# Head norms: sums of squares by two float32r products and 1/sqrt by logarithm, exponential and a Newton step

## The chip, the cores and the metric

The kernel runs on one core of one Trainium2 chip. The metric is the time of one launch in device microseconds (us). The core's engines are written as in the profile: PE is TensorE's matrix multiply and PEld its weight load, DVE is VectorE, ACT is ScalarE, POOL is GpSimd, and SP issues DMAs. Each engine works through its own list of instructions in order; between engines they wait on semaphores.

## What is computed

Four layers on a sequence of 512 tokens with 2048 channels. The first is a block with three branches side by side, then come an attention layer with a state space branch, a forgetting attention layer and a last norm. The change touches the first block alone, in three places, each a norm over the 64 channels of a head:

```python
# rwkv branch, 12 heads of 64: the key is brought to unit length per head
kk = (k * k_k).reshape(B, S, H, N)
kk = kk / jnp.maximum(jnp.sqrt(jnp.sum(jnp.square(kk), axis=-1, keepdims=True)), 1e-12)
...
_, y = lax.scan(step, jnp.zeros((B, H, N, N), f32), xs)
y = y.transpose(1, 0, 2, 3)
# ... and its output is normed per head
mu = jnp.mean(y, axis=-1, keepdims=True)
var = jnp.mean(jnp.square(y - mu), axis=-1, keepdims=True)
y = ((y - mu) * lax.rsqrt(var + GN_EPS)).reshape(B, S, C) * gn_g + gn_b      # GN_EPS = 64e-5
...
# stick-breaking attention, 12 heads of 64: q and k are normed per head
def _rms(x, g):
    y = xf * lax.rsqrt(jnp.mean(jnp.square(xf), axis=-1, keepdims=True) + RMS_EPS)   # 1e-6
q = _rms(heads(q), qn_g).astype(f32) * (HEAD_DIM ** -0.5)
k = _rms(heads(k), kn_g).astype(f32)
```

## The kernel before

Activations lie channel by token: a tile of 128 partitions holds 128 channels (two heads) of all 512 tokens, in float32. A dense product of a layer is a chain of steps, one for each 128 input channels. A step is three matmuls of 128x128 weights by 128x512 activations in float32r, since weights and activations are both split into a high and a low half: L310 is high by high, L311 and L312 are the mixed ones. The weights come from HBM in chunks of four steps (tile wr); the high half wh is a copy on ACT (L180) or on POOL (L279), the low half wl a subtraction on DVE (L162). L162, L175, L177 and L180 are helpers: two-operand arithmetic on DVE, an activation function on ACT without and with a bias operand, and a scaled copy on ACT.

The order of the work is written by Python generators. A dense product yields after each step, and `beside(main, side, wait)` advances a second generator by one piece for each piece of the first, from piece `wait` on. The smaller work of a head is thus dealt out between dense steps, and a `yield` in it means "one more dense step (or so) of the other stream first". What the program writes first stands first in each engine's list; nothing reorders it by cost. The rwkv branch runs six pairs of heads, j = 0 to 5, some 80 us each; `front(j + 1)` is dealt out beside the recurrence of pair j. Then the stick-breaking branch runs six pairs, some 59 us each, in the same manner.

`head_rs` is the function of the change. It takes one or two tiles of squares and a function `use` that applies the result, and it is called 18 times, all between 60 and 890 us of the span:

- six **key calls** (`front`, inside `decay`, one square, HEAD_LAG[0]). Just ahead of them `decay` makes two matmuls (L1398), two Tanh on ACT (L177), a linear step on DVE (L1401), a scan along time on DVE (L1402) and two Exp on ACT (L175); the square was made earlier.
- six **output norms** (`norm`, one square, HEAD_LAG[1]).
- six **stick calls** (`stick_front`, two squares, of q and of k, HEAD_LAG[2]), beside the dense product of v; after that product `turn` transposes v on PE (L1753), beside the product of the gate.

Before, a call makes for each square four float32 matmuls with the squares as weights and the 128x2 tile `heads` as data (L382; a float32 matmul stands in the trace as two records). That gives the sums with tokens on partitions, 8 numbers for each partition and square. On these `newton` works: a shift of the bits and three Newton steps, ten small instructions on DVE. L391 widens them to a full tile, the call yields HEAD_LAG times, and four float32 transposes for each square (L405) turn the tile back, to PSUM, where `use` reads it. Both PSUM tiles come from a ring of two (`early`).

Of the kernel before, what the change touches and what calls it, by code (L numbers as in the profile page):

```python
# [9 lines left out]
F32 = mybir.dt.float32  # L10
# [21 lines left out]
HEAD_LAG = (3,5,7)  # L32
# [108 lines left out]
class Kern:  # L141
# [49 lines left out]
    def constants(self, tmp):  # L191
# [33 lines left out]
        self.heads = c.tile([128, 2], F32, name="heads")  # L225
        V.tensor_copy(self.heads, blk[:, 0:128:64])
        self.ident_r = mr("ident_r")
        self.copy(self.ident_r, self.ident)
        self.one = c.tile([128, 1], F32, name="one")
# [132 lines left out]
    def small(self):  # L362
        return self.ps.tile([128, 512], F32, name="sm", bufs=4)
# [9 lines left out]
    def head_rs(self, pool, ring, sqs, ops, use, lag=4):  # L373


        nc = self.nc
        V = nc.vector
        n = 8 * len(sqs)
        ps = self.early()
        for i, sq in enumerate(sqs):  # L380
            for b in range(4):
                nc.tensor.matmul(ps[:, 8 * i + 2 * b:8 * i + 2 * b + 2], sq[:, 128 * b:128 * b + 128], self.heads,  # L382
                                 start=True, stop=True)
        small = lambda name, dt=F32: pool.tile([128, n], dt, name=name, bufs=2)
        m = small("hm")
        ops(m, ps[:, 0:n])
        y = self.newton(m, small("hy", I32), small("ht"))
        wide = []
        for i in range(len(sqs)):
            wide.append(ring())  # L390
            V.tensor_copy(wide[i].rearrange("p (g c) -> p g c", c=64),  # L391
                          y[:, 8 * i:8 * i + 8, None].to_broadcast([128, 8, 64]))
        for _ in range(lag):
            yield
        for i, t in enumerate(wide):
            ps = self.early()
            for b in range(4):
                n = slice(128 * b, 128 * b + 128)
                self.spread(ps[:, n], t[:, n])
            use(i, ps)  # L400
            yield
# [967 lines left out]
    def rwkv(self, pool, tm, yd, acts, rs):  # L1369
# [9 lines left out]
        def front(j):  # L1379
# [13 lines left out]
            def decay():  # L1393
# [17 lines left out]
                yield from self.head_rs(pool, tm, [sq], lambda m, s: V.tensor_scalar(m, s, 1e-24, None, op0=OP.max), use, HEAD_LAG[0])  # L1411
# [39 lines left out]
        def norm(j, g, bon, gate):  # L1451
# [16 lines left out]
            for _ in range(3):  # L1468
                yield
            yield from self.head_rs(pool, tb, [sq], lambda m, s: V.tensor_scalar(m, s, 1.0 / 64, 64e-5, op0=OP.mult,  # L1470
                                                                            op1=OP.add), use, HEAD_LAG[1])

# [448 lines left out]
```

## Time and profile before

| | |
|---|---|
| Time, median of three runs | 3025.04 us (3021.55 to 3025.70) |
| The profiled execution | 3014.29 us, of it 3012.5 us span |
| Mean granted clock of PE in it | 0.987 |
| PE busy | 97% of the span |
| DVE, ACT, POOL busy | 54%, 38%, 17% |
| The stretch of the 18 calls, 60 to 890 us | PE busy 804.0 us of 830.0 |

The profiled execution ran 10.75 us under the median. Its span goes from the first to the last instruction; 1.8 us lie around it. A row of a timeline gives the start from the span's start, the length, the engine, the line, what is written and read, and in brackets how long the engine stood idle before the row and what ended that. Rows of equal instructions are merged, with their count behind an x; the length is then that of all.

### The profile page before, as it was taken

The numbers are of one execution on the slowest core, as the hardware profiler recorded it, in microseconds if no ns is written. First come the engines' busy times: TensorE is split into PE (matmuls) and PEld (weight loads), VectorE is DVE, ScalarE is ACT, GpSimd is POOL, SyncE is SP. The second block draws the span as 40 slices with busy tenths as digits, with TensorE's granted clock in tenths as the row PEclk, the third lists the DMA queues.
The fourth block names the chain that finished last, engine by engine and source line by source line (L and its number), as shares of the span: only waits on it lengthen the run. The fifth ranks groups of instructions, "written<-read, shape, count | busy, mean of one in ns | idle before, by whom it ended". The sixth has DMA issues, their size and how long they took to land. (4 is left out here: it accounts for less than half of the span.)

```text
span 3012.5 us, 42942 instructions
## 1 busy us (share of the span) xinstructions
PE 2935.8 (97%) x16068; PEld 2400.4 (80%) x16068; DVE 1618.0 (54%) x3140; ACT 1134.9 (38%) x2043; POOL 498.8 (17%) x951
## 2 busy tenths in 40 slices
PE   7999999999999999999999999999999999999998
PEld 5777777878887777788888887878888888888887
DVE  7555555477667665655554456344444444444533
ACT  4444443354454223222344454233333232323432
POOL 4111111014764220211100000111101010100011
PEclk9999999999999999999999999999999999999999
DMA  4212122322235556455433325443333333323443
GB/s 141 64 59 60 55 60 69 95 75 84 90 95 167 155 163 196 133 158 157 138 105 103 104 85 177 147 130 109 101 105 96 98 96 97 95 92 95 147 122 119
DMA packets 195298, 334.03 MB, mean 111 GB/s; under 512 B 29696, under 2 KB 44672, under 8 KB 193936
## 3 DMA queue, kind: packets, MB, share of 16 engines
q1 hardware_dynamic: 193808, 327.08, 35.9%
q0 software_dynamic: 1280, 4.20, 0.4%
q8 instruction: 126, 2.06, 0.3%
q14 instruction: 84, 0.69, 0.1%
HBM read 289.55 MB, written 42.70 MB: 110 GB/s over the span
## 5 line engine op out<-in xcount | busy, mean ns | idle before, releaser
L310 PE MATMUL big<-hi,wh 128*128 128x512 f32 x3440 | 1375.7, 400 | 4.1 <-ACT hi L180 2.9
L312 PE MATMUL big<-hi,wl 128*128 128x512 f32 x3440 | 1350.9, 393 | 7.3 <-DVE wl L162 6.8
L311 PE MATMUL big<-lo,wh 128*128 128x512 f32 x3440 | 1349.1, 392 | 2.3 <-DVE lo L162 2.3
L162 DVE TENSOR_TENSOR wl<-wr,wh 128x512 fp32r<-128x512 f32 x884 | 648.3, 745 | 721.0 <-ACT wh L180 711.7
L312 PEld LDWEIGHTS big<-hi,wl 128*128 128x128 f32 x3440 | 649.6, 189 | 153.5 <-DVE wl L162 15.8
L310 PEld LDWEIGHTS big<-hi,wh 128*128 128x128 f32 x3440 | 649.7, 189 | 150.0 <-issue 10.7
L311 PEld LDWEIGHTS big<-lo,wh 128*128 128x128 f32 x3440 | 650.1, 189 | 133.2 <-DVE lo L162 5.6
L180 ACT ACTIVATE wh<-wr 128x512 fp32r<-128x512 f32 x820 | 505.8, 626 | 632.0 <-PE big L311 515.7
L1231 POOL TENSOR_SCALAR dm<-cb,cq 128x128 f32<-128x128 f32 (+1 forms) x64 | 42.4, 663 | 598.1 <-DVE mx L674 580.1
L680 ACT ACTIVATE pm<-pm,mx 128x128 f32<-128x128 f32 (+3 forms) x128 | 70.5, 552 | 178.1 <-DVE mx L676 178.1
L162 POOL TENSOR_TENSOR ssq<-ssq,sq 128x512 f32<-128x512 f32 (+1 forms) x43 | 54.6, 1269 | 380.1 <-ACT sq L175 359.5
L162 DVE TENSOR_TENSOR tm<-big,rs 128x512 f32<-128x512 f32 x86 | 59.2, 688 | 73.4 <-PE big L312 73.3
L175 ACT ACTIVATE sq<-xn 128x512 f32<-128x512 f32 (+1 forms) x47 | 28.8, 613 | 177.8 <-DVE xn L162 166.3
L279 POOL CAST wh<-wr 128x512 fp32r<-128x512 f32 x64 | 47.7, 747 | 143.5 <-PE big L311 93.0
L180 ACT ACTIVATE pt<-sm 128x512 f32<-128x512 f32 (+3 forms) x96 | 43.4, 526 | 62.7 <-PE sm L708 62.7
L162 DVE TENSOR_TENSOR xn<-big,xr 128x512 f32<-128x512 f32 (+1 forms) x50 | 33.3, 667 | 56.7 <-PE big L312 45.5
L1610 POOL MEMSET xi<- 64x16 f32 x6 | 0.7, 119 | 371.4 <-DVE xi L1609 371.4
L180 ACT ACTIVATE qk<-tm 128x512 fp32r<-128x512 f32 x32 | 20.2, 633 | 96.2 <-DVE tm L1366 48.1
L162 POOL TENSOR_TENSOR ssq<-xn 128x512 f32<-128x512 f32 x3 | 3.1, 1040 | 310.4 <-DMA wr<-w_out_even 143.5
L162 DVE TENSOR_TENSOR pl<-sm,pt 128x512 fp32r<-128x512 f32 (+1 forms) x48 | 25.9, 596 | 44.3 <-ACT pt L180 44.3
L686 DVE TENSOR_SCALAR pm<-pm,sm 128x128 f32<-128x128 f32 (+3 forms) x128 | 43.3, 400 | 1.1
L1366 DVE SCALAR_TENSOR_TENSOR tm<-big,rs 128x512 f32<-128x512 f32 x34 | 23.4, 689 | 36.9 <-PE big L312 36.9
(445 smaller groups left out, 3140.4 us busy)
## 6 DMA issues: line engine op xcount, KB each, us to landing
wr<-w_in_odd SPq DMA_DIRECT2D x256, 256.0 KB, 3.3
wr<-w_in SPq DMA_DIRECT2D x228, 256.0 KB, 3.1
wr<-w_in_even SPq DMA_DIRECT2D x192, 256.0 KB, 3.5
wr<-w_out SPq DMA_DIRECT2D x64, 256.0 KB, 3.8
wr<-w_out_even SPq DMA_DIRECT2D x64, 256.0 KB, 3.4
wr<-w_out_odd SPq DMA_DIRECT2D x64, 256.0 KB, 3.3
xr<-x SPq DMA_DIRECT2D x48, 256.0 KB, 3.0
yl<-y SPq DMA_DIRECT2D x45, 256.0 KB, 3.8
```

Of the source, the lines that this page charges most:

```text
L162: (eng or self.nc.vector).tensor_tensor(out, a, b, op=op)
L175: self.nc.scalar.activation(out, x, f, scale=scale)
L180: self.nc.scalar.activation(out, x, AF.Copy, scale=scale)
L279: self.nc.gpsimd.tensor_copy(wh, wr)
L310: nc.tensor.matmul(ps, wh[:, i], hi, start=(k == 0), stop=False)
L311: nc.tensor.matmul(ps, wh[:, i], lo, start=False, stop=False)
L312: nc.tensor.matmul(ps, wl[:, i], hi, start=False, stop=(k == n - 1))
L680: nc.scalar.activation(d, d, AF.Exp, bias=mx[:, b:b + 1], accum_out=sm[:, b:b + 1])
L686: V.tensor_scalar(d, d, sm[:, b:b + 1], None, op0=OP.mult)
L1231: nc.gpsimd.tensor_scalar(D[:, QOFF[b]:QOFF[b] + n], cb[:, 0:n], -1.0, cq[:, b, h:h + 1], op0=OP.mult, op1=OP.add)
L1366: self.nc.vector.scalar_tensor_tensor(t, ps, scale, rs, op0=OP.mult, op1=OP.mult)
L1610: G.memset(X.rearrange("p i c -> p (i c)")[:, 0:256:17], 1.0)
```

## The change

`head_rs` makes the sums as full tiles. The square is split into a high and a low half (a copy on ACT, a subtraction on DVE, tiles from the caller's ring). The call then yields HEAD_LAG times, and two float32r products of 128x512 with a 128x128 block matrix as weights give the sum (`blk_r`) or the mean (`mean_r`) of a head, spread over its 64 channels, in PSUM. 1/sqrt is exp(-0.5 ln): Ln on ACT (with the floor as bias; for the key calls DVE takes the maximum first), Exp on ACT, and one Newton step as three instructions on DVE, all on 128x512. `use` reads the result from SBUF. The small matmuls, `newton`'s part here, the widening copy and the transposes are gone; HEAD_LAG goes from (3, 5, 7) to (0, 4, 0).

```diff
-HEAD_LAG = (3,5,7)
+HEAD_LAG = (0,4,0)
...
-        self.heads = c.tile([128, 2], F32, name="heads")
-        V.tensor_copy(self.heads, blk[:, 0:128:64])
+        self.mean_r = mr("mean_r")
+        self.copy(self.mean_r, blk, scale=1.0 / 64)
...
-    def head_rs(self, pool, ring, sqs, ops, use, lag=4):
-        ps = self.early()
-        for i, sq in enumerate(sqs):
-            for b in range(4):
-                nc.tensor.matmul(ps[:, 8 * i + 2 * b:8 * i + 2 * b + 2], sq[:, 128 * b:128 * b + 128], self.heads,
-                                 start=True, stop=True)
...
-        m = small("hm")
-        ops(m, ps[:, 0:n])
-        y = self.newton(m, small("hy", I32), small("ht"))
...
+    def head_rs(self, ring, sqs, mat, op, floor, use, lag):
+        V = self.nc.vector
+        parts = []
+        for sq in sqs:
+            parts.append((ring(F32R), ring(F32R)))
+            self.split(*parts[-1], sq)
         for _ in range(lag):
             yield
-        for i, t in enumerate(wide):
-            ps = self.early()
-            for b in range(4):
-                n = slice(128 * b, 128 * b + 128)
-                self.spread(ps[:, n], t[:, n])
-            use(i, ps)
+        first = []
+        for sq, (hi, lo) in zip(sqs, parts):
+            ps = self.sums(self.early(), hi, lo, mat)
+            y, t = sq, ring()
+            if op == OP.add:
+                self.act(y, ps, AF.Ln, bias=self.floors[floor])
+            else:
+                V.tensor_scalar(y, ps, floor, None, op0=op)
+                self.act(y, y, AF.Ln)
+            first.append((ps, y, t))
+        for _, y, _ in first:
+            self.act(y, y, AF.Exp, scale=-0.5)
+        for i, (ps, y, t) in enumerate(first):
+            V.scalar_tensor_tensor(t, y, -0.5, y, op0=OP.mult, op1=OP.mult)
+            V.scalar_tensor_tensor(t, ps, floor, t, op0=op, op1=OP.mult)
+            V.scalar_tensor_tensor(y, t, 1.5, y, op0=OP.add, op1=OP.mult)
+            use(i, y)
             yield
...
-                yield from self.head_rs(pool, tm, [sq], lambda m, s: V.tensor_scalar(m, s, 1e-24, None, op0=OP.max), use, HEAD_LAG[0])
+                yield from self.head_rs(tm, [sq], self.blk_r, OP.max, 1e-24, use, HEAD_LAG[0])
...
+            yield from self.head_rs(tb, [sq], self.mean_r, OP.add, 64e-5, use, HEAD_LAG[1])
...
+            self.head_rs(tm, [y for _, _, _, y in x], self.mean_r, OP.add, 1e-6, use, HEAD_LAG[2]), STICK_WAIT[0])
```

The diff moves the lines of the file by two to four: L310 to L312 of before are L314 to L316 of the changed kernel, L1398 is L1401, L1647 is L1649, L1741 is L1743. Three places in the engines' lists follow. In all of them tm stands for any tile of the ring of that name.

PE at the fourth key call: two matmuls of `decay`, a dense step, and the first PE work of `head_rs`. Before:

```order
L312 MATMUL big<-hi,wl 128x512
L1398 MATMUL pa<-wdad,up 128x512 x2
L310 MATMUL big<-hi,wh 128x512
L311 MATMUL big<-lo,wh 128x512
L312 MATMUL big<-hi,wl 128x512
L382 MATMUL pa<-heads,tm 128x2 x4
L1647 MATMUL sm<-xb,GT 32x32 x32
L310 MATMUL big<-hi,wh 128x512
```

In the changed kernel:

```order
L316 MATMUL big<-hi,wl 128x512
L1401 MATMUL pa<-wdad,up 128x512 x2
L314 MATMUL big<-hi,wh 128x512
L315 MATMUL big<-lo,wh 128x512
L316 MATMUL big<-hi,wl 128x512
L422 MATMUL pa<-tm,blk_r 128x512
L423 MATMUL pa<-tm,blk_r 128x512
L1649 MATMUL sm<-xb,GT 32x32 x32
```

The two products (L422, L423) stand where the four small matmuls (L382) stood, one dense step and no more behind `decay`'s matmuls. Before, the transposes followed three dense steps further on; in the changed kernel nothing more of the call is on PE.

ACT at the same call, before: `decay`'s Tanh pair (L177) and Exp pair (L175), and what follows them:

```order
L180 ACTIVATE wh<-wr 128x512 x2
L177 ACTIVATE tm<-pa,half_w_147 128x512
L177 ACTIVATE tm<-pa,half_a_145 128x512
L175 ACTIVATE tm<-tm 128x512 x2
L180 ACTIVATE xb<-sm,m_110 64x512
L180 ACTIVATE wh<-wr 128x512
L177 ACTIVATE tm<-tm,oka,half_k_a 128x512
```

In the changed kernel:

```order
L180 ACTIVATE wh<-wr 128x512 x2
L177 ACTIVATE tm<-pa,half_w_151 128x512
L177 ACTIVATE tm<-pa,half_a_149 128x512
L175 ACTIVATE tm<-tm 128x512 x2
L180 ACTIVATE tm<-tm 128x512
L175 ACT_TABLE_LOAD
L175 ACTIVATE tm<-tm 128x512
L175 ACT_TABLE_LOAD
L175 ACTIVATE tm<-tm 128x512
L180 ACTIVATE xb<-sm,m_110 64x512
L177 ACTIVATE tm<-tm,oka,half_k_a 128x512
```

The copy of the square's high half (L180, tm from tm) stands behind the Exp pair, and Ln and Exp, each behind a table load, stand ahead of the copy to xb. In the whole of ACT's list table loads go from 31 to 66.

DVE at the fourth stick call, before: from the widening copy (L391) on, with the applications to q and k (L1741), the scores' arithmetic (sbe) and v's product coming out of PSUM (tm from big):

```order
L391 COPY tm<-hy 128x512 x2
L162 TENSOR_TENSOR wl<-wr,wh 128x512
L162 TENSOR_TENSOR sbe<-sbe,sm 128x512 x2
L162 TENSOR_TENSOR sbe<-sbe,sm 128x256
L162 TENSOR_TENSOR wl<-wr,wh 128x512
L162 TENSOR_TENSOR sbe<-sbe,m_lt 128x3x128
L162 TENSOR_TENSOR sbe<-sbe,m_lt 128x128
L1741 SCALAR_TENSOR_TENSOR RKV<-tm,qg_151,pa 128x512
L162 TENSOR_TENSOR q_7760<-RKV,q_7760 64x512
L162 TENSOR_TENSOR q_7763<-RKV,q_7763 64x512
L162 TENSOR_TENSOR tm<-big,rs 128x512
L1741 SCALAR_TENSOR_TENSOR RKV<-tm,pvt,pa 128x512
```

In the changed kernel, from the Newton step for k to the same row of v:

```order
L400 SCALAR_TENSOR_TENSOR tm<-tm 128x512
L401 SCALAR_TENSOR_TENSOR tm<-pa,tm 128x512
L402 SCALAR_TENSOR_TENSOR tm<-tm 128x512
L1743 SCALAR_TENSOR_TENSOR RKV<-tm,pvt 128x512
L162 TENSOR_TENSOR kl_5876<-RKV,k_7518 64x512
L162 TENSOR_TENSOR kl_5877<-RKV,k_7522 64x512
L162 TENSOR_TENSOR sbe<-sbe,sm 128x512 x2
L162 TENSOR_TENSOR sbe<-sbe,sm 128x256
L162 TENSOR_TENSOR wl<-wr,wh 128x512
L162 TENSOR_TENSOR sbe<-sbe,m_lt 128x3x128
L162 TENSOR_TENSOR sbe<-sbe,m_lt 128x128
L162 TENSOR_TENSOR tm<-big,rs 128x512
```

v's product comes out of PSUM (tm from big) behind the whole chain of k, its low halves (kl) and a further piece of the scores' arithmetic; before it stood ahead of k's application. Ahead of the rows shown stand, in the changed kernel, the two low halves of the squares and the same four instructions (L400 to L402, L1743) for q.

## Rows read from the trace of the kernel before

**Rows 1.** The page's first part: busy us (share of the span) xinstructions.

```profile
PE 2935.8 (97%) x16068; PEld 2400.4 (80%) x16068; DVE 1618.0 (54%) x3140; ACT 1134.9 (38%) x2043; POOL 498.8 (17%) x951
```

**Rows 2.** Groups of PE, 60-890 us: count, busy us, mean ns, idle before.

```profile
L382 PE MATMUL pa<-heads,tm 128*128 128x2 f32 x144 | 17.7, 249 | 8.0 <-ACT tm L177 5.5 <-ACT tm L175 2.4
...
L405 PE MATMUL pa<-ident,tm 128*128 128x128 f32 x72 | 11.3, 298 | 0.9 <-DVE tm L391 0.8
...
L382 PE MATMUL pa<-heads,tb 128*128 128x2 f32 x48 | 6.4, 256 | 0.0
...
L405 PE MATMUL pa<-ident,tb 128*128 128x128 f32 x24 | 3.6, 272 | 0.0
```

**Rows 3.** PE's waits, 60 to 890 us: in total, times, longest.

```profile
PE pa L1753 <- DVE tm L162: 2.9, 3, 1.2
```

**Rows 4.** Timeline, fourth key call: start us, length us, instruction [idle before].

```profile
261.06 1.13 PE L1398 MATMUL pa<-wdad,up 64*128 64x512 f32 x4
...
263.50 0.69 ACT L177 ACTIVATE tm<-pa,half_w 128x512 f32<-128x512 f32 x1
...
264.24 1.05 PE L382 MATMUL pa<-heads,tm 128*128 128x2 f32 x8 [1.16 <-ACT tm L177]
...
265.10 0.41 DVE L1401 TENSOR_SCALAR tm<-tm 128x512 f32<-128x512 f32 x1
...
265.54 1.22 DVE L1402 TENSOR_TENSOR_SCAN tm<-reset,tm 128x512 f32<-128x512 bf16 x1
...
266.80 1.29 ACT L175 ACTIVATE tm<-tm 128x512 f32<-128x512 f32 x2 [2.04 <-DVE tm L1402]
```

**Rows 5.** Timeline, the second output norm, just ahead of that call.

```profile
248.70 0.95 PE L382 MATMUL pa<-heads,tb 128*128 128x2 f32 x8
...
250.93 0.63 ACT L180 ACTIVATE wh<-wr 128x512 fp32r<-128x512 f32 x1 [1.81 <-PE big L311]
...
254.36 0.82 ACT L177 ACTIVATE tb<-tb,pvt 128x512 f32<-128x512 f32 x1 [2.80 <-DVE tb L162]
...
257.19 0.68 DVE L162 TENSOR_TENSOR tm<-big,rs 128x512 f32<-128x512 f32 x1
```

**Rows 6.** Groups of ACT and DVE, 60-890 us, columns as in Rows 2.

```profile
L175 ACT ACT_TABLE_LOAD x12 | 15.4, 1283 | 0.2
...
L1741 DVE SCALAR_TENSOR_TENSOR RKV<-tm,pvt,pa 128x512 f32<-128x512 f32 x6 | 4.4, 738 | 0.0
```

**Rows 7.** Timeline: a pair of float32r products over all channels.

```profile
154.08 0.39 PE L419 MATMUL pa<-tm,blk_r 128*128 128x512 f32 x1
...
154.30 0.40 PE L420 MATMUL pa<-tm,blk_r 128*128 128x512 f32 x1
```

**Rows 8.** Timeline: a table load and what follows it on ACT.

```profile
618.20 1.28 ACT L177 ACT_TABLE_LOAD   x1
...
619.49 1.28 ACT L177 ACTIVATE sbl<-sbl 128x1280 f32<-128x1280 f32 x1
```

**Rows 9.** Timeline, fourth stick call.

```profile
748.82 0.61 ACT L175 ACTIVATE tm<-tm 128x512 f32<-128x512 f32 x1
...
749.67 1.84 PE L382 MATMUL pa<-heads,tm 128*128 128x2 f32 x16
...
757.61 1.28 ACT L175 ACTIVATE sbe<-sbe 128x1280 f32<-128x1280 f32 x1 [7.66 <-DVE sbe L162]
...
765.21 0.69 DVE L162 TENSOR_TENSOR tm<-big,rs 128x512 f32<-128x512 f32 x1
...
766.04 0.63 PE L1753 MATMUL pa<-ident,tm 128*128 128x128 f32 x4 [1.21 <-DVE tm L162]
```

**Rows 10.** Timeline, second stick call.

```profile
629.34 1.05 PE L382 MATMUL pa<-heads,tm 128*128 128x2 f32 x8 [1.80 <-ACT tm L175]
...
634.86 0.21 ACT L175 ACTIVATE cn<-s5x 128x32 f32<-128x32 f32 x1
```

**Rows 11.** Stretch: PE, PEld, DVE, ACT, POOL busy (x), PE clock, DMA share, GB/s.

```profile
266.00:269.40 3.40, 3.40 (x35) 2.75 (x28) 3.02 (x14) 2.57 (x5) 0.00 (x0) 0.50 0.44 143
```

More of the change, by code (lines that the diff above doesn't have):

```diff
@@ L224, in constants @@
         V.scalar_tensor_tensor(self.cen_r, blk, -1.0 / 64, self.ident, op0=OP.mult, op1=OP.add)
-        self.heads = c.tile([128, 2], F32, name="heads")
-        V.tensor_copy(self.heads, blk[:, 0:128:64])
+        self.mean_r = mr("mean_r")
+        self.copy(self.mean_r, blk, scale=1.0 / 64)
         self.ident_r = mr("ident_r")
         self.copy(self.ident_r, self.ident)
+        self.floors = {}
+        for f in (1e-6, 64e-5):
+            self.floors[f] = c.tile([128, 1], F32, name="floor%d" % len(self.floors))
+            V.memset(self.floors[f], f)
         self.one = c.tile([128, 1], F32, name="one")
@@ L371, in silu @@
         self.nc.vector.scalar_tensor_tensor(g, t, 1.0, half, op0=OP.add, op1=OP.mult)
-    def head_rs(self, pool, ring, sqs, ops, use, lag=4):
-        nc = self.nc
-        V = nc.vector
-        n = 8 * len(sqs)
-        ps = self.early()
-        for i, sq in enumerate(sqs):
-            for b in range(4):
-                nc.tensor.matmul(ps[:, 8 * i + 2 * b:8 * i + 2 * b + 2], sq[:, 128 * b:128 * b + 128], self.heads,
-                                 start=True, stop=True)
-        small = lambda name, dt=F32: pool.tile([128, n], dt, name=name, bufs=2)
-        m = small("hm")
-        ops(m, ps[:, 0:n])
-        y = self.newton(m, small("hy", I32), small("ht"))
[L388 to L392, printed above, removed]
+    def head_rs(self, ring, sqs, mat, op, floor, use, lag):
[4 more added lines that the diff above has]
+            self.split(*parts[-1], sq)
         for _ in range(lag):
             yield
-        for i, t in enumerate(wide):
-            ps = self.early()
-            for b in range(4):
-                n = slice(128 * b, 128 * b + 128)
-                self.spread(ps[:, n], t[:, n])
-            use(i, ps)
+        first = []
[15 more added lines that the diff above has]
+            use(i, y)
             yield
@@ L1469, in norm @@
                 yield
-            yield from self.head_rs(pool, tb, [sq], lambda m, s: V.tensor_scalar(m, s, 1.0 / 64, 64e-5, op0=OP.mult,
-                                                                            op1=OP.add), use, HEAD_LAG[1])
+            yield from self.head_rs(tb, [sq], self.mean_r, OP.add, 64e-5, use, HEAD_LAG[1])
         finish(front(0))
@@ L1746, in stick_front @@
             self.projected(tm, 45 + j, acts, rs),
-            self.head_rs(self.fr, tm, [y for _, _, _, y in x],
-                         lambda m, s: V.tensor_scalar(m, s, 1.0 / 64, 1e-6, op0=OP.mult, op1=OP.add), use, HEAD_LAG[2]), STICK_WAIT[0])
+            self.head_rs(tm, [y for _, _, _, y in x], self.mean_r, OP.add, 1e-6, use, HEAD_LAG[2]), STICK_WAIT[0])
         def turn():
```

## The prediction, made before the changed kernel was run

> **What bounds the kernel now.** I read the page's first part for the bound, then PE's groups and waits between 60 and 890 us, where all 18 calls lie, then the timeline around one call of each sort. PE is busy for 97% of the span, DVE for 54% and ACT for 38% [rows 1]. So a call costs what it puts on PE, plus what PE waits for it; DVE's and ACT's part counts only where PE stands waiting at its end. Hardly any waiting is there now: before the sums 8.0 us in all, before the transposes 0.9 [rows 2], before the turn of v 2.9 [rows 3]. The call's chain is long, but its DVE part is small instructions, and PE does dense steps meanwhile.
>
> **PE's work.** Away go the sums and transposes, 17.7 + 11.3 + 6.4 + 3.6 = 39.0 us busy [rows 2]. A record runs on while the next matmul has begun: of a pair of products the first lasts 0.39 and the second starts 0.22 later [rows 7], so each of the 36 groups of sums and transposes gives back about 0.17 less: 39.0 - 6.1 = 32.9. In come 24 x 2 products of 0.22 each, 10.6. Net **-22.3**. Bounds: -28.4 without the 0.17, -14 if each product takes its whole record of 0.39. I take the pitch, since the products stand among dense steps.
>
> **Waits that go with the old form.** 8.0 + 0.9 + 2.9 = **-11.8** [rows 2, 3]. They belong to instructions that go, or to the turn, which I price anew below.
>
> **Key calls, the direct wait.** Before, the sums needed only the square, which is early. In PE's list the products stand at the same place, one dense step behind `decay`'s matmuls. But their operands are made at that point of the program, so ACT's list has the high half behind the Exp pair, which waits for Tanh, the linear step and the scan. In the fourth call Exp starts at 266.80 and lasts 1.29, to 268.09 [rows 4]. The copy takes 0.63 [rows 5] and the subtraction 0.69 (a DVE pass) [rows 5]: products at 269.4. PE was at this place at 264.24 - 1.16 = 263.1 [rows 4]. The wait is 6.3 us, and PE can't pass it, since its list is in order. Queued behind it are the small matmuls L1647 and the next dense steps, and nobody fills the gap.
>
> **Key calls, the chain ahead.** Calls three to six follow an output norm by some 10 us, and ACT and DVE do both in order. The norm's products themselves I cost at nothing: four yields, some 2.7 us of dense steps at 0.22 a matmul, cover the split of 1.3. Their consequence is on ACT. In the second norm ACT's copy at 250.93 ends at 251.56 [rows 5]; behind it come a table load of 1.28 [rows 6], Ln 0.63, a second load of 1.28, Exp 0.63: 255.4. Then DVE has three steps and the application at about 0.70 each, to 258.2, and L177 of 0.82 ends at 259.05. Before it ended at 254.36 + 0.82 = 255.18 [rows 5]: 3.9 later. The key's product coming out of PSUM (257.19) stands on DVE behind what L177 feeds, and from there shift, square, Tanh, scan and Exp follow closely, so all move by 3.9. PE arrives 0.7 earlier, its norm being cheaper. Wait 6.3 + 3.9 + 0.7 = 10.9 each, four of them 43.6; the first two calls have no norm ahead, and by the same reading of their own Exp I get 5.5 and 4.7, about 10 together. Sum **+53.6**. Bounds: 35 without the shift (four of 6.3 and the 10), 65 if the shift reaches the first two as well.
>
> **Key calls, what is late next.** Behind the products DVE has the maximum, three wide steps and the application, about 3.5, and ACT Ln, a load and Exp, 2.5, where before there were ten small instructions and a copy. What feeds `xb` and the bonus stands behind them. I take 2.4 a call, **+14**; bounds 0 (dense steps cover it) and 24 (4 each, the whole difference).
>
> **Stick calls, the products.** HEAD_LAG[2] is 0, so the low halves are made right where the products want them. In the fourth call PE arrives at 749.67; k's square ends at 749.43 [rows 9], a weight copy and two high halves of 0.6 follow on ACT, then DVE's last low half: about 2.2 of wait. Fourth to sixth are alike, 6.6. In the second call the high halves stand on ACT behind the scores' Exp, a table load and the sine pair, which ends at 634.86 + 0.21 [rows 10]. Before, PE could already start k's sums at 629.34, after a wait of 1.80; now the products end at about 637.5 and the wait is 10.0. The third call comes to 3.8, the first to 0.5. Together 20.9.
>
> **Stick calls, the turn.** v's product comes out of PSUM on DVE, and in the changed list that stands behind q's and k's chains and a piece of the scores. In the fourth call: products end 752.8, Ln of both 753.8, load 755.1, Exp of both 756.4, q's four DVE steps 758.7, its halves 761.2, a weight half, k's four steps 764.7, its halves 767.4, the scores' subtraction 769.0, their Exp of 1.28 (before at 757.61) [rows 9] 770.3, masks and weight halves 772.4, v 773.1. Before, v came at 765.21 and the turn began at 766.04 [rows 9]. PE, then 1.21 early, now some 0.5 to 0.9 later, waits 7.4. Fourth to sixth 22.1, third 7.1, second 4.0, first 0: 33.2. Stick sum **+54.1**, bounds 24 (only the products, and the turn as before at 2.9) and 75.
>
> **PE's clock.** Behind the fourth key call, 266 to 269.4, the granted clock was 0.50 of full, 1.2 GHz [rows 11]; such a stretch of 3.4 us costs 1.7. Before it stood a wait of 1.16 and matmuls of two columns. With a wait of 5 to 11 us in some 16 calls I expect about four stretches more, **+7**; bounds -3 (two go with the small matmuls) and +20 (twelve more).
>
> **Sum.** -22.3 - 11.8 + 53.6 + 14 + 54.1 + 7 = **+94.6**. The profiled execution of 3014.29 would become about 3109; the median lay 10.75 above that execution, so I add to it: 3025.04 + 94.6 = **3120**.
>
> A trace row against a rule: a table load lasts 1.283 [rows 6], and the ACTIVATE behind it starts 0.01 after the load's end (618.20 + 1.28, then 619.49) [rows 8]. The Trainium skill, page "ScalarE: Activation LUTs", section "What ACT_TABLE_LOAD costs", gives 1283 ns and a drain of about 1380 ns on top for each switch. By the row no drain stands on the path; by the page each of some 12 exposed loads would cost 1.38 more, an estimate of +17, so 3137. I go by the row.
>
> **Rivals.**
>
> *The other side: the halves are ready in time.* If the split and 1/sqrt of all calls lay beside dense steps after all, only the work and the old waits would move: -22.3 - 11.8 = -34.1, so 2991. It decides in favour of faster if the high half is there before PE has done the one dense step, that is if ACT's copy isn't bound behind Exp. ACT's busy share of 38% speaks for it, the lists against: an engine with idle time still works in order, and ACT's list has the copy behind Exp. 3%.
>
> *Only the direct waits.* The norm's chain ends before the key's shift wants ACT, v's evacuation is covered, and later steps hide the rest: key 35, stick 20.9 and the turn's old 2.9, no clock loss: -34.1 + 35 + 20.9 + 2.9 = +24.7, so 3050. For it speaks that DVE has 46% idle; against it that the rows of ACT from the shift to the Exp pair follow each other closely. 12%.
>
> *One load instead of two.* If Ln and Exp of a call ran with one table in place, some 11 exposed loads of 1.28 go: -14, so 3106. The changed kernel's list shows a load ahead of both, and 35 more in all. 4%. The Trainium skill, same page, section "Table sets: the hidden batching unit", names a set that holds exp and ln together, by which one load would do.
>
> *More than I see.* With DVE and ACT in arrears weight halves come late too, between the calls, and the upper bounds of clock and late steps hold: some 35 more, 3155. Weight halves stand on the very queues that get longer; against it, the chunks' ring of four. 13%.
>
> *That the change isn't in the built kernel* I exclude: its lists show products, loads and the missing transposes.
>
> **How the numbers follow.** Forecast 3120 with 66%, rivals as given, 2% for the rest. The range reaches down to the direct waits alone, 3050, and up to the last rival with half its surplus over the forecast again, 3170; the other side and the far ends stay out. A measurement of this kernel can tell about 0.2%, 6 us, from no change: three runs lay within 4.2. Faster 3%, same 1%, slower 96%.
>
> **What would show it.** PE's waits of the changed kernel should list the key products behind DVE's low half with about 54 us (four near 11, two near 5), the stick products near 21, the turn behind DVE near 33, and the loads' group should be at more than twice its count. If the key products wait for less than 3 us each, the other side holds; if the four late key calls wait near 6, the chain ahead is wrong; if the turn waits as before, v is covered. If the time is off with all waits as said, the clock or weight halves carry the rest.

## The result, and the profile after

| | before | changed |
|---|---|---|
| Median | 3025.37 us (4 runs, 3021.55 to 3028.54) | 3111.10 us (4 runs, 3106.51 to 3125.45) |
| Ratio, 95% interval | | 1.0298 (1.0271 to 1.0325) |
| The profiled execution, its span | 3014.29, 3012.5 | 3125.45, 3123.7 |
| Mean granted clock in it | 0.987 | 0.966 |

The change costs 2.98% of the time, 86 us by the medians. The profiled execution of the changed kernel was the longest of its four; the other three had a mean clock of 0.970 to 0.973. Its difference from that of before is therefore 111 us, and the rows below explain these 111; of the 25 us by which this is more than 86, the clock's share is named with the terms.

The page's first part, to be held against [rows 1]:

```profile
PE 2955.1 (95%) x15828; PEld 2404.5 (77%) x15828; DVE 1643.5 (53%) x3021; ACT 1222.9 (39%) x2151; POOL 501.6 (16%) x951
```

PE's busy time went up by 19 us although it has less to do, since a matmul at the half clock is busy for longer; ACT's went up by 88. In PE's groups, 60 to 1000 us (columns as in [rows 2]), the products stand where the sums stood:

```profile
L423 PE MATMUL pa<-tm,blk_r 128*128 128x512 f32 x12 | 7.2, 601 | 0.5 <-DVE tm L162 0.5
...
L422 PE MATMUL pa<-tm,blk_r 128*128 128x512 f32 x12 | 7.0, 580 | 47.5 <-ACT tm L180 47.5
...
L423 PE MATMUL pa<-tm,mean_r 128*128 128x512 f32 x12 | 6.4, 535 | 3.0 <-DVE tm L162 3.0
L1754 PE MATMUL pa<-ident,tm 128*128 128x128 f32 x24 | 6.2, 410 | 37.3 <-DVE tm L162 37.3
...
L422 PE MATMUL pa<-tm,mean_r 128*128 128x512 f32 x12 | 5.9, 491 | 13.3 <-ACT tm L180 13.3
```

The busy time of the sums, transposes and `newton` is gone, and the idle time before the key products (blk_r) is 48.0 us, of it 1.4 before a bonus product, before the stick products (mean_r from tm) 16.3, before the turn (L1754) 37.3. Beside the six calls' own products, the group of key products holds six of the branch's bonus term (those of [rows 7]), and that of stick products the second square of each call. The output norms' products (mean_r from tb) wait for nothing.

The timeline of the fourth key call of the changed kernel shows the chain that PE stands at the end of, as [rows 4] did before:

```profile
284.40 1.13 PE L1401 MATMUL pa<-wdad,up 64*128 64x512 f32 x4
...
290.87 0.67 ACT L177 ACTIVATE tm<-pa,half_w 128x512 f32<-128x512 f32 x1
...
291.44 0.67 ACT L177 ACTIVATE tm<-pa,half_a 128x512 f32<-128x512 f32 x1
...
292.98 1.23 DVE L1405 TENSOR_TENSOR_SCAN tm<-reset,tm 128x512 f32<-128x512 bf16 x1
294.24 1.29 ACT L175 ACTIVATE tm<-tm 128x512 f32<-128x512 f32 x2 [2.13 <-DVE tm L1405]
295.43 0.61 ACT L180 ACTIVATE tm<-tm 128x512 fp32r<-128x512 f32 x1
...
296.08 0.69 DVE L162 TENSOR_TENSOR tm<-tm 128x512 fp32r<-128x512 f32 x1 [1.88 <-ACT tm L180]
...
296.10 0.79 PE L422 MATMUL pa<-tm,blk_r 128*128 128x512 f32 x1 [9.68 <-ACT tm L180]
...
296.82 0.79 PE L423 MATMUL pa<-tm,blk_r 128*128 128x512 f32 x1
```

Tanh, scan, Exp, high half: they follow each other closely, with the linear step between Tanh and scan. The first product (296.10) starts when the high half is done, 9.68 us after PE had come to it, and the second (296.82) when the low half is done. The Tanh pair is late because of the output norm ahead, whose own chain is this one (before: [rows 5]):

```profile
274.75 1.28 ACT L177 ACT_TABLE_LOAD   x1
...
275.66 0.39 PE L422 MATMUL pa<-tb,mean_r 128*128 128x512 f32 x1
...
276.32 0.69 ACT L177 ACTIVATE tb<-pa,floor 128x512 f32<-128x512 f32 x1 [0.29 <-PE pa L423]
...
277.03 1.28 ACT L175 ACT_TABLE_LOAD   x1
...
278.33 0.63 ACT L175 ACTIVATE tb<-tb 128x512 f32<-128x512 f32 x1
...
278.99 0.69 DVE L400 SCALAR_TENSOR_TENSOR tb<-tb 128x512 f32<-128x512 f32 x1 [3.53 <-ACT tb L175]
...
281.90 0.82 ACT L177 ACTIVATE tb<-tb,pvt 128x512 f32<-128x512 f32 x1 [2.94 <-DVE tb L162]
```

The load ahead of Ln (274.75) lies beside the products and costs nothing, Ln waits for the second product; the one ahead of Exp (277.03) is in the chain for its whole length. From the products' start to the shift (L177) it takes 6.2 us, where before it took 5.7 from the sums (248.70 to 254.36). The chain as such is thus 0.6 longer; what moved it more is its place. The four yields now lie ahead of the products, which start 8.7 us ahead of `decay`'s matmuls (275.66 to 284.40), where the sums started 12.4 us ahead of them (248.70 to 261.06). Against those matmuls the shift is 4.2 us later. Whether fewer yields ahead of the norm's products would give some of it back no run tests.

Last, the turn of the fourth stick call, with v's evacuation (tm from big) behind the scores' masks (before: [rows 9]):

```profile
852.00 0.69 DVE L162 TENSOR_TENSOR wl<-wr,wh 128x512 fp32r<-128x512 f32 x1 [1.85 <-ACT wh L180]
852.62 0.75 DVE L162 TENSOR_TENSOR sbe<-sbe,m_lt 128x384 f32<-128x384 f32 x2
...
853.29 0.68 DVE L162 TENSOR_TENSOR tm<-big,rs 128x512 f32<-128x512 f32 x1
...
854.02 1.12 PE L1754 MATMUL pa<-ident,tm 128*128 128x128 f32 x4 [8.76 <-DVE tm L162]
```

And the clock behind the fourth key call (columns as in [rows 11]), first the wait with what precedes it, then the 16 us after, then the rest of the round:

```profile
284.40:296.10 11.70, 2.02 (x9) 0.78 (x8) 6.35 (x10) 7.67 (x15) 0.00 (x0) 0.80 0.34 95
296.10:312.00 15.90, 15.90 (x188) 12.09 (x189) 9.41 (x17) 6.21 (x8) 0.00 (x0) 0.61 0.06 19
312.00:373.00 61.00, 58.79 (x493) 46.08 (x492) 29.18 (x49) 28.29 (x52) 8.47 (x29) 0.97 0.16 52
```

In those 16 us PE is busy throughout, at a mean clock of 0.61, that is 12 of them at 1.2 GHz.

### The profile page after: what moved, and what is told of

It reads as the page before. It is cut to its first block, busy times and chain, and to the rows that moved or that the text cites. A ratio compares the mean times of both kernels' runs of the same rounds, so it can differ in the third digit from the quotient of the medians.

```text
span 3123.7 us, 42446 instructions
## 1 busy us (share of the span) xinstructions
PE 2955.1 (95%) x15828; PEld 2404.5 (77%) x15828; DVE 1643.5 (53%) x3021; ACT 1222.9 (39%) x2151; POOL 501.6 (16%) x951
## 5 line engine op out<-in xcount | busy, mean ns | idle before, releaser
L314 PE MATMUL big<-hi,wh 128*128 128x512 f32 x3440 | 1385.7, 403 | 4.3 <-ACT hi L180 3.8
L316 PE MATMUL big<-hi,wl 128*128 128x512 f32 x3440 | 1357.8, 395 | 6.2 <-DVE wl L162 5.7
L316 PEld LDWEIGHTS big<-hi,wl 128*128 128x128 f32 x3440 | 655.5, 191 | 154.5 <-DVE wl L162 13.4
L314 PEld LDWEIGHTS big<-hi,wh 128*128 128x128 f32 x3440 | 655.8, 191 | 152.1 <-issue 10.7
L180 ACT ACTIVATE wh<-wr 128x512 fp32r<-128x512 f32 x820 | 505.5, 626 | 637.3 <-PE big L315 524.7
L175 ACT ACTIVATE sq<-xn 128x512 f32<-128x512 f32 (+1 forms) x47 | 28.8, 613 | 178.0 <-DVE xn L162 166.5
L180 ACT ACTIVATE pt<-sm 128x512 f32<-128x512 f32 (+3 forms) x96 | 43.5, 525 | 62.7 <-PE sm L711 62.7
L180 ACT ACTIVATE qk<-tm 128x512 fp32r<-128x512 f32 x32 | 20.3, 633 | 96.3 <-DVE tm L1369 48.1
L422 PE MATMUL pa<-tm,blk_r 128*128 128x512 f32 x12 | 7.0, 580 | 47.5 <-ACT tm L180 47.5
L175 ACT ACTIVATE tm<-tm 128x512 f32<-128x512 f32 (+1 forms) x60 | 37.0, 626 | 35.5 <-DVE tm L1405 11.0
```

Source lines behind the costliest of these rows:

```text
L175: self.nc.scalar.activation(out, x, f, scale=scale)
L180: self.nc.scalar.activation(out, x, AF.Copy, scale=scale)
L314: nc.tensor.matmul(ps, wh[:, i], hi, start=(k == 0), stop=False)
L316: nc.tensor.matmul(ps, wl[:, i], hi, start=False, stop=(k == n - 1))
```

## The experiments

All are built on the changed kernel unless it is said otherwise. The time before, on the chips of these runs, was 3020 to 3024 us in the median. Where a kernel's lines are numbered otherwise, L423, L426, L454 or L478 are its first product of a pair, and L1757, L1760, L1786 or L1810 its turn.

### Key calls: halves split early (e1_key_early)

```diff
             self.act(sq, kk, AF.Square)
+            kparts = [(tm(F32R), tm(F32R))]
+            self.split(*kparts[0], sq)
...
-self.head_rs(tm, [sq], self.blk_r, OP.max, 1e-24, use, HEAD_LAG[0])
+self.head_rs(tm, [sq], self.blk_r, OP.max, 1e-24, use, HEAD_LAG[0], kparts)
```

> The changed kernel with one edit: in the key calls the square is split right behind Square, ahead of decay's work, instead of behind its Exp pair. My theory (PE waits for the high half because ACT's list has it behind Exp): the products no longer wait for Exp, but still for a PSUM tile of the ring of two, which decay's Tanh pair sets free; behind an output norm that pair is 3.9 us late. So the four late key calls wait about 6 us instead of 9.7 and the first two about 1 instead of 4.6 and 2.8; sum 26 instead of 47.5, and with some 8 us less at the half clock about 3080 us. Rival (the wide steps and table loads of the calls hold up DVE and ACT as such, wherever the split stands): key waits stay within 5 us of 47.5, time 3105 to 3115.

Measured: 3122.23 us, ratio 1.0320 (1.0292 to 1.0348). The key waits came out as expected, from 60 to 1000 us (columns as in [rows 3]):

```profile
PE pa L423 <- ACT tm L177: 27.3, 6, 5.9
```

27.3 us, and the releaser is Tanh (L177), which frees the PSUM tile, and no longer the high half. The order of ACT's queue is thus what PE had waited for. But the time did not fall; it lies above both numbers, mine and the rival's. Behind the wait stands this stretch (columns as in [rows 11]):

```profile
290.60:310.00 19.40, 17.98 (x187) 13.89 (x188) 11.38 (x21) 8.21 (x12) 0.00 (x0) 0.50 0.17 55
```

For 19.4 us the clock was at half, against 12 in the changed kernel. Of the 3.8 us by which the fourth call's products came earlier, 0.3 were left nine dense steps further on: from the start of `decay`'s matmuls to the end of the ninth dense step behind the products it took 27.7 us, in the changed kernel 28.0.

Nor did the whole gain come off PE's waits. The key waits fell by 20.2 us, all of PE's idle time by 9.8 (151.8 to 142.0). New among the waits is one for the copy to xb, which on ACT now stands right behind the call's two table loads, Ln and Exp:

```profile
PE sm L1662 <- ACT xb L180: 5.0, 4, 1.2
```

Another 4.0 us are new before a weight half, and the turn waits 2.4 longer. So about half of the gain came back as other waits, the first of them by the rival's mechanism, and the clock took the rest: the loss at half clock went up from 74.0 to 85.0 us.

### Needless products in the wait (e6_fill, e6b_fill12, e13_early_fill16)

```diff
-            ps = self.sums(self.early(), hi, lo, mat)
+            ps = self.early()
+            for _ in range(fill[0] if fill else 0):
+                self.nc.tensor.matmul(ps, mat, fill[1], start=True, stop=True)
+            self.sums(ps, hi, lo, mat)
...
+... use, HEAD_LAG[0], (0 if j < 2 else 38, acts[0][0]))     # e6; 12 in e6b; 16 in e13, on top of e1
```

> The changed kernel with 38 needless products of 128x512 ahead of the key products in the four late key calls; they need nothing that is late, write the same PSUM tile and take about 8.4 us of the 9.7 us wait. Theory (PE's idle time brings the half clock that follows it): the wait before the products falls to 1 to 3 us, and the stretches at 0.50 behind the four calls, some 12 us each after the wait, vanish or shrink to 3.4; 15 to 24 us less, about 3090 us. Rival (the half clock comes from something else, or the added work only costs): 3108 or more, stretches as before.

Measured: 3132.10 us, ratio 1.0353 (1.0326 to 1.0380), slower by 21 us than the changed kernel, and not faster. I had overlooked that the needless products want the PSUM tile too: they start when Tanh frees it, 5.2 us into the wait, and 38 of them then run beyond the end of the wait. The half clock behind did shrink, from 17 to 20 us to 6.8 (3.4 at the last call), the wait's last part included. The number was wrong, so it was made smaller.

> As e6_fill, with 12 needless products of 128x512 ahead of the key products in the four late key calls, not 38. They can start when Tanh frees the PSUM tile, some 5.2 us into the wait, and should be done when the halves are ready, so the wait's end does not move. Theory (the half clock is kept up by what PE does after the wait, and dense products end it): the stretches at 0.50 behind the four calls end some 10 us sooner than in the changed kernel, 4 to 6 us are saved in each, time 3085 to 3098. Rival (the clock does not follow PE's work): stretches as before, 3108 or more.

Measured: 3110.30 us, ratio 1.0296 (1.0279 to 1.0314): no gain. The products of the fourth call started 12.5 us after `decay`'s matmuls (11.7 without the filling), nearly as meant. The stretch behind:

```profile
286.20:302.00 15.80, 15.18 (x197) 11.93 (x198) 10.07 (x18) 8.61 (x12) 0.00 (x0) 0.82 0.11 36
```

The clock is 0.82 from the first needless product on. The half clock ended 5.8 us behind that product, where in the changed kernel it ended 12.3 us behind the first key product, and the ninth dense step ended after 24.1 us, where the same calls take 26.1 in e2_stick_lag9 (whose code up to the stick calls is that of the changed kernel) and 28.0 in the profile of the changed kernel. So 2 to 4 us a call are won at that place. Over a whole round, from one `decay` to the next, little is left: 85.1 us here, 85.4 in e2_stick_lag9, 88.9 in the profile of the changed kernel. In three of the four rounds a further stretch of 3.4 us at half, worth 1.7, stands in the recurrence some 60 us later; in e2_stick_lag9 it stands in none of these four. The rows bear out that the half clock ends sooner when dense work follows; the size that I expected, 4 to 6 us in each of four calls, they do not.

> The kernel with the early split of the key squares, and 16 needless products of 128x512 ahead of the key products in the four late key calls, behind the same wait of 5.9 us. This is to tell why the early split brought no gain. Theory (behind the shorter wait PE goes on with 2 products and 64 matmuls of 32 columns, and so stays at the half clock for 20 us): with 16 products first the stretches at 0.50 shrink from 20.5 to 10 us or less; each costs 4 to 6 us of work and saves about 5, so 3110 to 3125, with the granted clock up from 0.964 to 0.970 or more. Rival (the early split lost its gain elsewhere, in DVE's or ACT's queues): stretches stay near 20, time 3135 to 3145.

Measured: 3109.76 us, ratio 1.0295 (1.0278 to 1.0312), mean clock 0.975 in the profile.

```profile
288.70:306.00 17.30, 16.72 (x206) 12.86 (x205) 10.00 (x18) 7.54 (x11) 0.00 (x0) 0.85 0.10 33
```

With 16 products more than in e1, PE was through the ninth dense step 2.0 us sooner than there (25.7 instead of 27.7), and the kernel was 12 us faster than e1. Between the two profiles the loss at half clock falls by 33.8 us (85.0 to 51.2), against 19.6 more work and 4.7 more waits. So what e1's other waits had left of its gain was lost to the clock. Why the clock stays down longer behind e1's wait of 5.9 us than behind one of 9.7 stays open. Part of it is the execution: behind the same waits of 9.7 the profile of the changed kernel has 17.1 to 20.5 us at half and that of e2_stick_lag9 13.7. And e5 (below) has a wait of 5.6 us, the same instructions behind it, and 10.2 us at half. One difference is in the rows: e1's stretch holds the second wait, of 1.2 us before L1662, which neither e5 nor the changed kernel has. That it keeps the clock down is not shown.

### Without the added table loads (e4_no_ln)

```diff
-                self.act(y, ps, AF.Ln, bias=self.floors[floor])
+                self.act(y, ps, AF.Tanh, bias=self.floors[floor])
...
-                self.act(y, y, AF.Ln)
+                self.act(y, y, AF.Tanh)
...
-            V.scalar_tensor_tensor(t, y, -0.5, y, op0=OP.mult, op1=OP.mult)
+            V.scalar_tensor_tensor(t, y, 0.0, y, op0=OP.mult, op1=OP.mult)
...
-            V.scalar_tensor_tensor(y, t, 1.5, y, op0=OP.add, op1=OP.mult)
+            V.scalar_tensor_tensor(y, t, 0.0, y, op0=OP.add, op1=OP.mult)
```

> The changed kernel with Tanh in the place of Ln and two factors 0 in the Newton step, so that the norms come out as 0: all instructions stay, but no call needs another table, 31 loads instead of 66. It leaves out the value of 1/sqrt. My theory (a load counts only where the chain behind it ends a wait: the load ahead of Ln lies beside the products, the one ahead of Exp is exposed): 1.3 us less in each of four late key calls and five turns, about 12 together, and a few for the clock, about 3095 us. Rival (all 35 added loads of 1.28 count): 45 us less or more, 3066 or under. By the Trainium skill's drain the difference would be twice as large as mine, about 24.

Measured: 3105.71 us, ratio 1.0271 (1.0242 to 1.0300).

```profile
PE pa L422 <- ACT tm L180: 42.9, 7, 8.5
...
PE sm L1649 <- DVE xb L1639: 4.5, 2, 2.7
...
PE pa L1754 <- DVE tm L162: 29.1, 5, 7.7
```

The key waits fell from 47.5 to 42.9 (9.7 to 8.5 in each of the four late calls), L1649's from 5.8 to 4.5, the turn's from 37.3 to 29.1: together 14.1, expected 12. A late key wait fell by 1.17, one load's length and no more. So of the 35 loads added, 45 us on ACT, some 14 are in the path, and neither the rival nor a drain behind each load is borne out. The median fell by 5 us and not by the 16 expected, inside the spread of the runs; between the two profiled executions, whose mean clocks were 0.966 and 0.967, the time fell by 17.8.

### One sort of call at a time in the old form (e5_norm_old, e7_key_old, e9_key_norm_old)

```diff
+    def head_rs_old(self, pool, ring, sqs, ops, use, lag=4):      # head_rs of before, word for word
...
+self.head_rs_old(pool, tb, [sq], ..., use, 5)      # norms: e5, e9
+self.head_rs_old(pool, tm, [sq], ..., use, 3)      # key calls: e7, e9
```

> The changed kernel with the output norms done in the old form (small matmuls, newton, transposes, five yields), key and stick calls new. My theory (the norm's two loads, Ln, Exp and wide steps come 3.9 us too late for the key chain behind them): the four late key calls wait about 6 us instead of 9.7, 15 less. PE has some 4 us more work. What the clock does with a shorter wait is open, since with the key squares split early a wait of 5.9 was followed by a longer stretch at the half clock than one of 9.7: between 3095 and 3115 us. Rival (the norm does not hold up the key call): late key waits stay at 9.7.

Measured: 3099.89 us, ratio 1.0256 (1.0236 to 1.0276). In the timeline, the fourth key call:

```profile
290.38 0.79 PE L454 MATMUL pa<-tm,blk_r 128*128 128x512 f32 x1 [5.57 <-ACT tm L180]
```

5.57 us instead of 9.68, the releaser still the high half: the direct wait alone, and the 4 us come from the norm's new form, its place and its chain together.

> The changed kernel with the key calls in the old form (lag 3), output norms and stick calls new. The sums then need the early square, and wait only for the PSUM tile that Tanh frees, which the norm ahead still makes 3.9 us late. My theory: late key waits near 5.8 us, the first two near 1, together 25 instead of 47.5, as with the early split; 6 us more work on PE; time between 3085 and 3115, the clock deciding. Rival (the wide steps behind the key products were the cost, not the wait ahead of them): the time falls by over 40, under 3070.

Measured: 3086.37 us, ratio 1.0211 (1.0189 to 1.0233).

```profile
PE pa L417 <- ACT tm L177: 23.3, 6, 5.2
```

23.3 us for 25 expected, of it 5.2 in each of the four late calls. The waits are those of e1, and yet this kernel is 36 us faster than e1. Behind the wait PE does the old sums and transposes, PE does not wait at the place of L1662, and the half clock lasts 10.2 us in all instead of 20.5. In the whole profile 49.5 us are lost at half clock, in e1 85.0.

> Key calls and output norms in the old form, stick calls alone as in the change (lag 0). My theory: waits from 600 to 1000 us as in the changed kernel, 16 before the products and 37 before the turn, against 4.7 in the kernel before; PE's work 11 less; half clock some 12 us dearer; 3025 + 49 - 11 + 12 = about 3075 us. So of the 86 us that the change costs, some 50 come from the stick calls and the rest from key calls and norms together. Rival (the calls disturb each other and the shares don't add): under 3050 or over 3100.

Measured: 3072.72 us, ratio 1.0168 (1.0150 to 1.0185), for 3075 expected.

```profile
PE pa L1786 <- DVE tm L162: 38.5, 6, 9.0
PE pa L454 <- ACT tm L180: 13.2, 5, 9.0
```

The waits are those of the changed kernel. From the last three medians follow the shares of the 86 us: stick calls 52 (3072.7 less 3020.3), norms 14 (3086.4 less 3072.7), key calls 25 (3111.1 less 3086.4). They add up to 91, with the two medians of before 5 apart. For the norms e5 gives 11 by another way (3111.1 less 3099.9).

### Stick calls: products later, chain later (e2_stick_lag9)

```diff
-HEAD_LAG = (0,4,0)
+HEAD_LAG = (0,4,9)
```

> The changed kernel with HEAD_LAG (0, 4, 9) instead of (0, 4, 0): in the stick calls the products come nine dense steps behind their halves, which is behind v's product, so v's evacuation stands ahead of the whole chain on DVE. My theory: the products' wait falls from 16.3 us to under 3 and the turn's from 37.3 to under 5; with some 10 us less at the half clock about 3055 us. Rival (the chain only moves, and the scores or the weight halves behind it wait instead): the sum of PE's waits from 600 to 1000 us falls by less than 20, time 3090 or more.

Measured: 3107.46 us, ratio 1.0276 (1.0245 to 1.0307), against 3055 expected.

```profile
PE big L316 <- DVE wl L162: 24.5, 7, 5.8
...
PE pa L1754 <- DVE tm L401: 5.5, 4, 2.0
```

Turn and products hardly wait (5.5, and 3.7 in the one call with the sine pair), but a wait of 24.5 us for weight halves (wl) is new. The timeline of the third call shows it:

```profile
758.75 0.69 DVE L400 SCALAR_TENSOR_TENSOR tm<-tm 128x512 f32<-128x512 f32 x1
...
760.92 0.75 DVE L1743 SCALAR_TENSOR_TENSOR RKV<-tm,pvt 128x512 f32<-128x512 f32 x1
...
762.37 0.68 DVE L162 TENSOR_TENSOR kl<-RKV,k 64x512 fp32r<-64x512 f32 x1 [0.69 <-ACT k L180]
763.67 0.69 DVE L162 TENSOR_TENSOR kl<-RKV,k 64x512 fp32r<-64x512 f32 x1 [0.62 <-ACT k L180]
...
764.58 2.69 DVE L162 TENSOR_TENSOR wl<-wr,wh 128x512 fp32r<-128x512 f32 x4
...
765.32 0.79 PE L316 MATMUL big<-hi,wl 128*128 128x512 f32 x1 [5.78 <-DVE wl L162]
```

v is out of the way, but now k's three steps, its application and its low halves, each waiting on a copy on ACT, stand ahead of four weight halves that PE wants: 5.78 us. Waits from 570 to 1000 us fell by 20 and not by 45; the rival's mechanism. The median fell by 4 us only. The profiled execution was the fastest of its four by 11 us, at a mean clock of 0.973, where the others had 0.969 and 0.970.

### Stick calls: the chain dealt out (e11_stick_spread, e14_stick_sooner, e15_stick_sooner3)

Key calls and norms are in the old form here.

```diff
         for i, (ps, y, t) in enumerate(first):
             V.scalar_tensor_tensor(t, y, -0.5, y, op0=OP.mult, op1=OP.mult)
             V.scalar_tensor_tensor(t, ps, floor, t, op0=op, op1=OP.mult)
+            if thin:
+                yield
             V.scalar_tensor_tensor(y, t, 1.5, y, op0=OP.add, op1=OP.mult)
+            if thin:
+                yield
             use(i, y)
...
-HEAD_LAG = (0,4,0)
+HEAD_LAG = (0,4,8)       # e11: the chain beside the gate, the turn after it; 5 in e14, 3 in e15
...
-STICK_WAIT = (8,6)
+STICK_WAIT = (3,6)       # e14, e15: the chain beside v
```

> Key calls and output norms old; the stick calls with products, but their halves are made eight steps ahead beside v, the products come at the end of v, the chain behind them is dealt out in eight pieces beside the gate's product, and the turn comes after it. My theory (only the queue order costs): no wait before the products, v's evacuation ahead of the chain, PE's work 11 us less and the old waits of 4.7 gone: 3010 to 3020 us, at or just under the kernel before. Rival (the whole-tile steps on DVE hold up the weight halves, as with lag 9, where 24.5 us of waits for wl appeared): 15 to 25 us of waits for wl and 3035 to 3045.

Measured: 3038.74 us, ratio 1.0053 (1.0038 to 1.0069).

```profile
PE sm L808 <- ACT k L194: 18.0, 5, 4.5
...
PE pa L478 <- ACT tm L194: 3.0, 1, 3.0
```

Products and weight halves hardly wait (3.0 and 1.9), but the scores of the next pair of heads wait 18.0 us for k, which is now late. That was neither theory's.

> As e11_stick_spread (key calls and norms old, stick calls new and dealt out), but the halves are made from the third step of v's product on, the products come five steps later and the chain's pieces beside the rest of v; the turn as before six steps into the gate. Theory (the 18.0 us that the scores waited for k in e11 came from the late start): that wait falls under 5, the turn waits under 5; PE's work 11 less, 3012 to 3022 us, at or under the kernel before. Rival (the whole-tile steps don't fit beside the scores' arithmetic on DVE, wherever they start): the turn or weight halves wait 15 us or more, 3030 to 3045.

Measured: 3034.40 us, ratio 1.0046 (1.0032 to 1.0060).

```profile
PE pa L1810 <- DVE tm L176: 15.7, 5, 4.3
PE pa L478 <- ACT tm L194: 5.7, 4, 3.2
```

The scores' wait is gone, and the turn waits 15.7 us again, about 3.1 in five calls, since q's chain and k's Newton step stand ahead of v's evacuation on DVE: the rival's case. All of PE's idle time from 60 to 1000 us is 17 us more than before and its work 11 less, and some 10 more are lost at the half clock.

> As e14_stick_sooner, with the products three steps behind their halves instead of five. Theory: the products wait 1 to 2 us a call where five steps hid the split, the chain ends 1.4 us sooner; within 6 us of e14. Rival (the chain's end decides): 6 us or more faster than e14.

Measured: 3062.84 us, ratio 1.0140 (1.0120 to 1.0160).

```profile
PE pa L1810 <- DVE tm L176: 28.4, 5, 7.9
PE pa L478 <- ACT tm L194: 12.2, 5, 4.5
```

Two steps fewer cost 28 us, 12.7 of it in the turn and 6.5 before the products, which neither theory had. DVE's list tells why: with a chain that begins sooner v's evacuation stands behind k's low halves again, as in the changed kernel, where e14 has it ahead of k's application. No version tried beats the kernel before.

## Why the prediction was right, and where its terms were off

Forecast 3120 (3050 to 3170), measured 3111; slower as said. By terms, in us of the profiled executions. For the measured side PE's time in a span is cut in three: idle between its records (59.8 before, 151.8 after); lost at the half clock, which is half of the time at 0.50 in which it wasn't idle (32.8 and 74.0); and the rest, the work at full clock (2909.8 and 2887.8; the start before PE's first matmul is in it).

| Term | Predicted | Measured |
|---|---|---|
| PE's work | -22.3 | -22.0 |
| Old waits gone | -11.8 | -11.8 |
| Key products | +53.6 | +46.5 |
| What is late next | +14 | +6.1 |
| Stick products | +20.9 | +16.3 |
| Turn | +33.2 | +37.3 |
| PE's other waits | 0 | -2.4 |
| Half clock | +7 | +41.2 |
| Sum | +94.6 | +111.2 |

**The bound.** Right: what counts is PE's work and PE's waits. The 25 us of further work on DVE and the 88 on ACT as such cost nothing; where 45 of ACT's were taken away (e4) only the waits at the chain's ends moved.

**PE's work.** Right to 0.3 us, with the pitch of 0.22 for a product and the 0.17 of a record's tail.

**Key calls.** The mechanism was right in both parts and was shown apart: the high half behind Exp (e1: the releaser becomes Tanh), and the norm ahead (e5: 5.6 instead of 9.7). The late calls measured 9.7 for 10.9. The direct part is 5.6, where the prediction had 6.3: it counted the subtraction of 0.69 and expected DVE's low half to end the wait, but the first product needs the high half alone, and the rows name ACT's copy (47.5 us) and not DVE (0.5). The norm's part is 4.1 for 3.9 and 0.7. The first two had 4.6 and 2.8 for 5.5 and 4.7.

**What is late next.** Mis-sized: 6.1 for 14, namely 4.0 more before L1649, 1.4 before a bonus product and 0.6 before a product of the recurrence. The rest ends in no wait of PE. Before L1649 (L1647 before), first the kernel before, then the changed one:

```profile
PE sm L1647 <- DVE xb L1637: 1.8, 1, 1.8
```

```profile
PE sm L1649 <- DVE xb L1639: 5.8, 2, 3.9
```

**Stick calls.** Right in kind, 53.6 for 54.1. The turn was 8.8 to 9.0 in the last three for 7.4, the second call's product wait 8.9 for 10.0, and the last three calls' 1.2 to 1.5 for 2.2.

**The clock.** The step that failed: four further stretches of 3.4 us, +7, with an upper bound of +20. The stretch was read behind a wait of 1.16 us. In the profiled execution the term was +41.2, of it 36 between 60 and 1000 us: each of the 13 waits there of more than 2.7 us was followed by a stretch at half of 6.8 to 20.5 us, the wait's last part included. Of the other executions there are no rows. If PE's work and waits are the same in them, the 85.7 us between the medians leave 85.7 + 22.0 - 92.0, about +16, for the clock; the other three executions of the changed kernel did have a higher mean clock, 0.970 to 0.973 for 0.966. The waits were thus put 18 too high, and the clock 9 too low by the medians and 34 by the profiled executions; the sum came out 9 over by the medians and 17 under by the profiled executions. That the forecast is nearer than its terms is luck.

**The load's price.** By the row: 1.28 and no drain. e4 took the load ahead of Exp out of the late key calls and their wait fell by 1.17 each. The Trainium skill's sum of load and drain (page "ScalarE: Activation LUTs", section "What ACT_TABLE_LOAD costs"), some 2.66 us a switch, would have made it 2.7; the measurement differs, and it decides.

**The rivals.** The halves in time: no, by 48 us. Only the direct waits: no; the norm's chain and v's evacuation were both there. One load instead of two: the trace has two in each call, as at 274.75 and 277.03 above. Arrears in weight halves: not in the changed kernel, whose PE waits for none of them in that stretch; but it is what appears once the other waits are taken away (e2).

## What to carry to other kernels

An operation that takes less of the bound engine can cost more than it saves if its operands are made behind a long queue: look in the list of each engine for what stands ahead of the operand, not at the engine's busy share. Where a chain of small instructions is replaced by one of whole tiles, moving it moves the wait: here in turn to the products, the evacuation of v, the weight halves and the scores. And a wait of PE is to be priced with the clock behind it, from a stretch of the trace where PE waited for as long and went on with the same kind of work.

## What the runs showed of the hardware

- Behind waits of 5 to 10 us PE's clock was at 0.50 for 7 to 20 us, the wait's last part included, although PE was busy from the wait's end on. In the profile of the changed kernel the half clock ended 3 to 4 us after the wait's end at the stick calls, where dense steps follow (a loss of some 2 us each), and 12 to 13 us after it at the late key calls, where 64 matmuls of 32 columns and a few dense steps follow (some 6 us each).
- What PE does then matters, though it does not settle it alone. Behind a wait of 5.9 us, with 2 products and 64 matmuls of 32 columns first, the clock was at half for the whole 19.4 us shown, which hold a second wait of 1.2 (e1); with 16 products of 128x512 first, the mean of the 17.3 us shown was 0.85 (e13). But e5, with the former kind of work behind 5.6 us, had 10.2 us at half.
- The mean clock differs between executions of one kernel: 0.966 to 0.973 in four of the changed kernel, whose times differ by 19 us. And from 60 to 570 us, where e9, e11, e14 and e15 have the key calls and norms of the kernel before, they lost 18.8 to 25.6 us at half clock and the profile before 17.0. So a difference of less than some 9 us in one profile's clock tells nothing of a change.
- A table load costs its 1.28 us where the chain passes through it (1.17 off a late key wait in e4), nothing where it can run ahead beside other work: 14 us of waits for 45 us of loads.
